# Weight sums in another stage, the residual kept by groups of 768 tokens, and fixed places for the s tiles

## The chip, the cores and the metric

The kernel runs on one core of one Trainium2 chip. The metric is the device time of one execution in microseconds (us); the figure for a kernel is the median of its runs. The core's engines are TensorE (PE in the rows; PEld is its weight load), VectorE (DVE), ScalarE (ACT), GpSimd (POOL) and SyncE (SP), which here issues nearly all transfers, in one order.

## What is computed

Two requests, a prompt of 512 tokens and a sample of 1024, go through the same two layers in fp32: multi-head latent attention, then a chunked gMLP, each with a gate and a residual, and a last norm.

```python
def mla_layer(x, ...):                       # layer 1
    h = rmsnorm(x, g)
    q_lat, kv_lat, k_rope, gate = jnp.split(h @ w_in, [384, 640, 704], axis=-1)
    q  = (rmsnorm(q_lat, q_norm) @ w_q_up)   # 8 heads, 128 + 64
    kv = (rmsnorm(kv_lat, kv_norm) @ w_kv_up)
    ...                                      # rope, softmax over the whole sequence
    return x + (o * jax.nn.silu(gate)) @ w_out

def gmlp_layer(x, ...):                      # layer 2, width 2048
    h = rmsnorm(x, g)
    u, v, gate = jnp.split(h @ w_in, 3, axis=-1)
    u = jax.nn.gelu(u, approximate=False)
    v = layernorm(jax.nn.gelu(v, approximate=False), ln_g, ln_b)
    sv = ...                                 # per group of 256: w_s (128x128) times v, per chunk of 128 tokens
    s = u * sv.reshape(bsz, seq, 2048)
    return x + (s * jax.nn.silu(gate)) @ w_out
```

## The kernel before

Activations lie with channels on the 128 partitions and tokens along the row; a chunk is C = 512 tokens. The sample has the chunks g = 0 and 1, the prompt is g = 2. Every fp32 product is made of three products of a high and a low part: `mm3` multiplies the high weights by the high activations (the first of three lines, L145 in attention, L1232 in the gMLP's output), the high weights by the low activations (the second) and the low weights by the high activations (the third). `split` makes the two parts: ScalarE casts (L150 for activations, L63 for weights) and VectorE subtracts (L151, L64). So before TensorE can use a tile it needs a cast and then a subtract. TensorE turns a matmul of 128x512 around every 0.23 us.

The program is a list of steps; a framework places each instruction in the order of its engine, and from there every engine works in that order.

The stages, with their times in the profile: **a_in_s**, norm and input projection of the sample, 0 to 190 us; attention of the sample to about 575; the prompt's input projection, about 572 to 640; attention of the prompt to 795; **out_s**, the sample's output projection with its residual, to 873; **out_p**, the prompt's, to about 925; then the gMLP. It treats the 1536 tokens as two groups G of 768 (H = 384 is half a group): `b_v` makes v, `b_ug` makes u and the gate and multiplies to s, `b_out` is the output projection, by chunks again: `b_out(0)` from 1302, `b_ug(1)` to 1774, `b_out(1)` and `b_out(2)` from 1774 to 1963.

What the change and the prediction touch:

- **The weight sums.** The gMLP's products are formed by a scheme of seven products of block sums, so sums of blocks of the value weights wv are made once and kept in DRAM (`Sv`). `w_sums(u)` (L810) is one of 16 units: a load of 128x4x256 (`ws<-wv`, L819), four VectorE operations of 128x256 that build on each other (L825), a store (`sv<-ws`, L826). Units 0 to 7 stand in the prompt's input projection, one per step that uses a 'wa' weight; units 8 to 15 in out_s.
- **a_in_s.** `k_step(k, c)` loads a piece x of chunk c, makes its high part on ScalarE (`h_hi`, L287) and its low part on VectorE (`h_lo`, L288), squares it, and adds the squares up on GpSimd (`acc`, L225). TensorE sums the squares over partitions (`ps_st`, L201); VectorE fetches that as `ms` (L203, L163), GpSimd takes the power (`rstd`, L166), and TensorE spreads the result (`ps_bc`, L209), before it goes on.
- **Spread of a norm in the prompt's projection.** `ps_n` (L179, L180) is made from the high and low part (`sh`, `sl`) of a diagonal tile `dg` (L193), which VectorE fills from `rstd`. The rotary part loads a turned copy of the keys there (`rope<-kr`, L343).
- **out_p and the loads of the next group.** `AOut.out` loads a piece of the old residual (`x<-xp`, L746), adds the product to it (L750) and stores the new residual x1 (L751). `b_prep` loads x1 again as `hQ` (L896), in 24 pieces for a group, and spreads the norm as `ps_n` (L916, L917). x1 lies in DRAM as 3 x 8 tiles of 128x512.
- **s and b_out.** `end` (L1132, L1133) stores s to DRAM (`sd<-uo`). `s_load` (L1154) loads a tile of one of the 16 channel blocks d of a chunk into one of five temporary buffers and splits it into `sh`, `sl`. `b_out` runs over the outputs f and the halves u of d: f0u0, f1u0, f2u0, f0u1, and so on, 24 matmuls each. The split tiles live in a rotating pool. For the sample's second chunk three of them, d 0 to 2, are loaded and split within the last unit of `b_ug(1)`, into a pool of their own (`pre`):

```python
        npre = (0, 3)[G]
        b_ug(G, [s_load(G, d, npre) for d in range(npre)])
        step(lambda G=G: open_out(G))
        for d in range(npre, 8):
            step(s_load(G, d, npre))
```

Of the kernel before, what the change touches and what calls it, by code (L numbers as in the profile page):

```python
# [88 lines left out]
def trunk_kernel(tc, A):  # L89
# [293 lines left out]
    def a_in_s():  # L383
        a = AIn("s", 2)

        def begin():
# [346 lines left out]
    class AOut:  # L733
# [9 lines left out]
        def out(self, f, c):  # L743
# [66 lines left out]
    def w_sums(u):  # L810

        vu, kt, hf = u // 8, u // 2 % 4, u % 2
        o = slice(hf * 256, hf * 256 + 256)

        def load():
            t = st["wsum", u] = st["ws"].tile([128, 4, 256], F32, tag="ws", bufs=3 - vu, name="ws")
            nc.sync.dma_start(out=t, in_=A["wv"][vu][:, :, kt, o])  # L819

        def make():
# [325 lines left out]
    def s_load(g, d, pre=0):  # L1147
        def fn():
            x = tmp("s")
            t0 = g * C  # L1150
            while t0 < (g + 1) * C:
                G, o = divmod(t0, 2 * H)
                n = min(2 * H - o, (g + 1) * C - t0)
                nc.sync.dma_start(out=x[:, t0 - g * C:t0 - g * C + n], in_=st["sd", G, d][:, o:o + n])  # L1154
                t0 += n
            hl = [st["pre"].tile([128, C], F32R, name=f"s{e}{d}") if d < pre else
                  st["po"].tile([128, C], F32R, tag="s" + e, bufs=24 if g else 16, name="s" + e)
                  for e in "hl"]
            split(hl[0], hl[1], x)
            st["sf", g, d] = hl  # L1160
# [131 lines left out]

    def open_sums():
        if ("v2d", 0) not in st:
            b_dram()
        st["ws"] = open_pool("ws", side="right")

    def sums_at(n, us):

        if 0 <= n - 2 < len(us):  # L1300
            step(w_sums_of[us[n - 2]][1])
        if 0 <= n < len(us):
            step(w_sums_of[us[n]][0])

    w_sums_of = [w_sums(u) for u in range(16)]
# [22 lines left out]
    def open_out1():  # L1328
# [219 lines left out]
```

## Time and profile before

| | us |
|---|---|
| median of three runs | 1964.0 (1963.76, 1964.0, 1965.2) |
| profiled execution, its own time | 1964.92 |
| its span in the trace | 1963.1 |
| PE busy | 1918.7 (98% of the span) |
| DVE busy | 1294.8 (66%) |
| ACT busy | 889.9 (45%) |
| POOL busy | 140.6 (7%) |
| mean granted clock of TensorE | 0.991 of full |

The profiled execution is 0.9 us above the median of the runs. TensorE is busy for nearly the whole span, so the time is its work plus the few places where it waits, plus the places where its granted clock falls to half: such a stretch shows as 0.50 in the column PEclk of the windows, 1.2 GHz in place of 2.4. A matmul that is busy at half clock counts as busy, so the lost time there is not in the 2% of idle time.

### The profile page before, as it was taken

What the parts mean: (1) busy time and instruction counts of PE and PEld (TensorE: products, weight loads), DVE (VectorE), ACT (ScalarE), POOL (GpSimd) and SP (SyncE); (2) the same over time, 40 slices, a digit from 0 to 9 for tenths busy, and PEclk for the clock granted to TensorE, in tenths of its full rate; (3) what the DMA queues carried; (4) which work ended last, traced back from release to release, by engine and by line L of the source; (5) the groups of instructions that cost most, each with busy time, mean ns of one, the idle gap of its engine ahead of it and who ended that gap; (6) DMA issues with size and microseconds to landing.
All of it is one profiled execution on the core that took longest, in us unless ns stands there. A gap on an engine that the chain in (4) does not pass through costs nothing.

```text
span 1963.1 us, 26564 instructions
## 1 busy us (share of the span) xinstructions
PE 1918.7 (98%) x10226; PEld 1696.1 (86%) x10226; DVE 1294.8 (66%) x1990; ACT 889.9 (45%) x1382; POOL 140.6 (7%) x99
## 2 busy tenths in 40 slices
PE   8999999999998999998999999999999999999998
PEld 6888888888886888886889999988888999998887
DVE  7443777777877787747758777766655665656443
ACT  5322544454543555323544544553444454545321
POOL 5100000000011000122000000001100000000111
PEclk9999999999998999998999999989999999999999
DMA  5211000000126311765557655466575555546443
GB/s 162 86 39 58 27 13 22 17 28 17 38 77 213 107 47 63 235 226 188 183 169 237 199 183 182 157 208 199 160 257 187 190 171 186 165 137 224 167 166 102
DMA packets 127342, 269.42 MB, mean 137 GB/s; under 512 B 12400, under 2 KB 54896, under 8 KB 127216
## 3 DMA queue, kind: packets, MB, share of 16 engines
q1 hardware_dynamic: 127216, 267.73, 42.2%
q8 instruction: 80, 1.31, 0.3%
q14 instruction: 46, 0.38, 0.1%
HBM read 198.74 MB, written 65.01 MB: 134 GB/s over the span
## 4 chain that ended last, share of the span: by engine, by line
PE 85%; DVE 7%; DMA 4%; issue 2%; ACT 1%; POOL 0%; SPq 0%; POOLq 0%; DVEq 0%; ACTq 0%
PE s L595 9%; PE mm L145 7%; PE mm L146 7%; PE mm L147 7%; PE X L984 6%; PE X L985 6%; PE X L986 6%; PE mm L1233 4%; PE mm L1232 4%; PE mm L1234 4%; PE pst L627 3%; PE Z L985 3%; PE Z L984 3%; PE Z L986 3%; PE sv L1118 2%; PE o L146 2%
## 5 line engine op out<-in xcount | busy, mean ns | idle before, releaser
L63 ACT CAST w_hi<-w_raw 128x1024 fp32r<-128x1024 f32 (+3 forms) x267 | 261.0, 978 | 383.2 <-PE mm L146 101.9
L64 DVE TENSOR_TENSOR w_lo<-w_raw,w_hi 128x1024 fp32r<-128x1024 f32 (+3 forms) x267 | 304.5, 1141 | 187.3 <-ACT w_hi L63 186.7
L225 POOL TENSOR_TENSOR acc<-acc,sq 128x512 f32<-128x512 f32 x70 | 115.7, 1654 | 1456.5 <-ACT sq L223 574.8
L1233 PE MATMUL mm<-sl,w_hi 128*128 128x512 f32 (+1 forms) x416 | 157.0, 377 | 2.9 <-DVE sl L151 2.9
L1232 PE MATMUL mm<-sh,w_hi 128*128 128x512 f32 (+1 forms) x416 | 156.3, 376 | 1.9 <-ACT sh L150 1.9
L1234 PE MATMUL mm<-sh,w_lo 128*128 128x512 f32 (+1 forms) x416 | 156.5, 376 | 0.0
L610 ACT ACTIVATE p<-s,sm 128x1024 f32<-128x1024 f32 (+1 forms) x96 | 93.3, 974 | 103.9 <-DVE sm L606 103.8
L150 ACT CAST pth<-pst 128x512 fp32r<-128x512 f32 x160 | 86.5, 591 | 67.2 <-PE pst L627 65.2
L145 PE MATMUL mm<-h_hi,w_hi 128*128 128x512 f32 x288 | 114.8, 399 | 1.0 <-ACT rbc L310 0.9
L147 PE MATMUL mm<-h_hi,w_lo 128*128 128x512 f32 x288 | 113.2, 393 | 0.0
L146 PE MATMUL mm<-h_lo,w_hi 128*128 128x512 f32 x288 | 113.1, 393 | 0.0
L604 DVE TENSOR_REDUCE sm<-s 128x1 f32<-128x1024 f32 (+1 forms) x80 | 97.6, 1220 | 19.5 <-PE s L595 19.4
L151 DVE TENSOR_TENSOR ptl<-pst,pth 128x512 fp32r<-128x512 f32 x160 | 104.7, 683 | 8.4 <-ACT pth L150 8.3
L994 ACT COPY t<-X 128x384 f32<-128x384 f32 (+1 forms) x88 | 44.5, 511 | 126.0 <-PE X L986 125.1
L1233 PEld LDWEIGHTS mm<-sl,w_hi 128*128 128x128 f32 x416 | 79.1, 190 | 18.5 <-DVE sl L151 4.6
L1232 PEld LDWEIGHTS mm<-sh,w_hi 128*128 128x128 f32 x416 | 79.2, 190 | 16.3 <-ACT sh L150 2.2
L1234 PEld LDWEIGHTS mm<-sh,w_lo 128*128 128x128 f32 x416 | 79.2, 190 | 13.9
L146 PE MATMUL o<-ptl,vh 128*128 128x256 f32 x320 | 91.1, 285 | 0.0
L147 PE MATMUL o<-pth,vl 128*128 128x256 f32 x320 | 91.0, 284 | 0.0
L145 PE MATMUL o<-pth,vh 128*128 128x256 f32 x320 | 90.2, 282 | 0.0
L984 PE MATMUL X<-gbh,w_hi 128*128 128x384 f32 x256 | 85.9, 335 | 3.3 <-DVE uo L1083 3.2
L984 PE MATMUL X<-gah,w_hi 128*128 128x384 f32 x256 | 86.9, 339 | 0.0
(292 smaller groups left out, 5112.5 us busy)
## 6 DMA issues: line engine op xcount, KB each, us to landing
w_raw<-wbo SPq DMA_DIRECT2D x50, 512.0 KB, 3.4
w_raw<-wug SPq DMA_DIRECT2D x48, 512.0 KB, 4.4
w_raw<-sv SPq DMA_DIRECT2D x32, 512.0 KB, 3.7
su<-su SPq DMA_DIRECT2D x32, 512.0 KB, 4.1
w_raw<-su SPq DMA_DIRECT2D x32, 512.0 KB, 4.8
w_raw<-wa SPq DMA_DIRECT2D x25, 512.0 KB, 3.6
w_raw<-wv SPq DMA_DIRECT2D x24, 512.0 KB, 3.6
v2d<-c SPq DMA_DIRECT2D x48, 256.0 KB, 2.5
```

The lines of the kernel that those rows point to most:

```text
L63: self.nc.scalar.copy(hi[:, :n], raw[:, :n])
L64: self.nc.vector.tensor_tensor(out=lo[:, :n], in0=raw[:, :n], in1=hi[:, :n].bitcast(F32), op=ALU.subtract)
L145: pe.matmul(out, lh, rh, start=(i == 0), stop=False)
L146: pe.matmul(out, lh, rl, start=False, stop=False)
L147: pe.matmul(out, ll, rh, start=False, stop=(i == n - 1))
L595: pe.matmul(s[:, j2 * C:(j2 + 1) * C], l[:, o], r[:, cc], start=(j == 0), stop=(j == 4))
L984: pe.matmul(ps, lh, rh, start=first, stop=False, skip_group_check=True)
L985: pe.matmul(ps, lh, rl, start=False, stop=False, skip_group_check=True)
L986: pe.matmul(ps, ll, rh, start=False, stop=last, skip_group_check=True)
L1232: pe.matmul(ps, wh[:, ksl(kk)], sh, start=(k == 0), stop=False)
L1233: pe.matmul(ps, wh[:, ksl(kk)], sl, start=False, stop=False)
L1234: pe.matmul(ps, wl[:, ksl(kk)], sh, start=False, stop=(k == 15))
```

## The change

- **Sums.** `w_sums` has 8 units of 128x4x512 in place of 16 of 128x4x256. The first four are moved from the prompt's input projection to a_in_s (`sums_at` after `k_step(k, 1)` from k = 2 on, one at every second step, and on into the steps that follow); the other four stay in out_s, at every third step, with one buffer. The pool `ws` is opened at the start of a_in_s, and the pool of the latents takes its place at (f, c) = (5, 0).
- **Residual.** x1 lies in DRAM as 2 x 8 tiles of 128x768, one for each group G. `by_group` cuts a range of tokens at the group's bound. The stores of the sample's second chunk and the loads of it in `b_out(1)` come in two pieces; the `hQ` loads of a group are 8 of 128x2x384 in place of 24.
- **s tiles.** They get fixed places by tags, allocated in `open_out` in an order that puts d 4 to 12 over memory of h2b, 0 to 3 over `vin` and `sv`, and 13 to 15 over `sv` and `uo`. For g = 2, d 0 to 7 get places of their own, and d 8 to 15 the places 0 to 7. The early load and split of three tiles in the last unit of `b_ug(1)` and their pool are gone; d 0 to 7 are all loaded after `open_out`.

```diff
     def w_sums(u):
-        vu, kt, hf = u // 8, u // 2 % 4, u % 2
-        o = slice(hf * 256, hf * 256 + 256)
+        vu, kt = divmod(u, 4)
         def load():
-            t = st["wsum", u] = st["ws"].tile([128, 4, 256], F32, tag="ws", bufs=3 - vu, name="ws")
-            nc.sync.dma_start(out=t, in_=A["wv"][vu][:, :, kt, o])
+            t = st["wsum", u] = st["ws"].tile([128, 4, C], F32, tag="ws", bufs=2 - vu, name="ws")
+            nc.sync.dma_start(out=t, in_=A["wv"][vu][:, :, kt, :])
...
         for k in range(KD):
             step(k_step(k, 1))
+            sums_at(k - 2, 0, 2)
             if k == 2:
                 step(lambda: a.stats1(0))
...
                 step(lambda f=f, c=c: a.mm(f, c), ("wa", f))
+                sums_at(2 * f + c, 0, 2)
+                if (f, c) == (5, 0):
+                    step(open_lats)
...
+    def sums_at(n, u0, every):
+        u, i = divmod(n, every)
+        if i == 0 and 0 <= u < 4:
+            step(w_sums_of[u0 + u][0])
+        u, i = divmod(n - 2, every)
+        if i == 0 and 0 <= u < 4:
+            step(w_sums_of[u0 + u][1])
...
-    n = 0
-    for s in mm_p[1:2] + mm_p[3:]:
-        step(*s)
-        if len(s) > 1 and s[1][0] == "wa":
-            if n == 0:
-                step(open_sums)
-            sums_at(n, range(8))
-            if n == 9:
-                step(lambda: close_pool("ws"))
-            n += 1
+    steps(mm_p[1:2] + mm_p[3:])
...
-            nc.sync.dma_start(out=st["x1d", g, f], in_=x)
+            for d, o in by_group("x1d", f, g * C, C):
+                nc.sync.dma_start(out=d, in_=x[:, o])
...
-                    t0, t1 = 2 * H * G, 2 * H * (G + 1)
-                    while t0 < t1:
-                        g, o = divmod(t0, C)
-                        h, q = divmod(t0 - 2 * H * G, H)
-                        n = min(C - o, H - q, t1 - t0)
-                        nc.sync.dma_start(out=Q[k][:, j + 2 * h, q:q + n],
-                                          in_=st["x1d", g, k + 4 * j][:, o:o + n])
-                        t0 += n
+                    nc.sync.dma_start(out=Q[k][:, j:j + 3:2, :], in_=st["x1d", G, k + 4 * j].rearrange(
+                        "p (a b) -> p a b", a=2))
...
-            unit(2 * p + 1, AF.Silu, g, early if p == 7 else ((), (), norm_v(p + 1)))
+            unit(2 * p + 1, AF.Silu, g, ((), (), norm_v(p + 1)) if p < 7 else ())
...
+    def s_tiles(g, d):
+        i = d if g < 2 else d + 16 if d < 8 else d - 8
+        st["sf", g, d] = [st["po"].tile([128, C], F32R, tag=f"s{e}{i}", bufs=1, name="s" + e) for e in "hl"]
...
+        for d in (*range(4, 13), *range(4), *range(13, 16)):
+            s_tiles(G, d)
...
-        npre = (0, 3)[G]
-        b_ug(G, [s_load(G, d, npre) for d in range(npre)])
+        b_ug(G)
         step(lambda G=G: open_out(G))
-        for d in range(npre, 8):
-            step(s_load(G, d, npre))
+        for d in range(8):
+            step(s_load(G, d))
```

How the orders of two engines change at three places. First, VectorE in a_in_s while the last pieces of the second chunk are split (`h_lo`) and the norm's sum is fetched (`ms`). Before:

```order
L151 TENSOR_TENSOR w0lo<-w0raw,w0hi 128x128 x3
L288 SCALAR_TENSOR_TENSOR h_lo_1_342<-x,vec,h_hi_1_341 128x512
L288 SCALAR_TENSOR_TENSOR h_lo_1_360<-x,vec,h_hi_1_359 128x512
L288 SCALAR_TENSOR_TENSOR h_lo_1_378<-x,vec,h_hi_1_377 128x512
L288 SCALAR_TENSOR_TENSOR h_lo_1_406<-x,vec,h_hi_1_405 128x512
L288 SCALAR_TENSOR_TENSOR h_lo_1_424<-x,vec,h_hi_1_423 128x512
L288 SCALAR_TENSOR_TENSOR h_lo_1_454<-x,vec,h_hi_1_453 128x512
L288 SCALAR_TENSOR_TENSOR h_lo_1_463<-x,vec,h_hi_1_462 128x512
L288 SCALAR_TENSOR_TENSOR h_lo_1_472<-x,vec,h_hi_1_471 128x512
L203 COPY ms<-ps_st 128x4
```

After, the end of the same piece:

```order
L299 SCALAR_TENSOR_TENSOR h_lo_1_412<-x,vec,h_hi_1_411 128x512
L844 TENSOR_TENSOR ws<-ws 128x512
L299 SCALAR_TENSOR_TENSOR h_lo_1_430<-x,vec,h_hi_1_429 128x512
L844 TENSOR_TENSOR ws<-ws 128x512
L299 SCALAR_TENSOR_TENSOR h_lo_1_460<-x,vec,h_hi_1_459 128x512
L299 SCALAR_TENSOR_TENSOR h_lo_1_478<-x,vec,h_hi_1_477 128x512
L844 TENSOR_TENSOR ws<-ws 128x512 x4
L299 SCALAR_TENSOR_TENSOR h_lo_1_515<-x,vec,h_hi_1_514 128x512
L299 SCALAR_TENSOR_TENSOR h_lo_1_524<-x,vec,h_hi_1_523 128x512
L844 TENSOR_TENSOR ws<-ws 128x512
L299 SCALAR_TENSOR_TENSOR h_lo_1_540<-x,vec,h_hi_1_539 128x512
L203 COPY ms<-ps_st 128x4
```

Seven operations of the sums stand in this piece between the `h_lo` and ahead of `ms`, and an eighth just ahead of the piece.

Second, VectorE in the prompt's input projection, from the key's scaling (`kr`) to the diagonal tile `dg` that the spread of the norm needs. Before:

```order
L336 TENSOR_TENSOR kr<-mm,rbc_5589 128x512
L64 TENSOR_TENSOR w_lo<-w_raw,w_hi 128x1024
L825 TENSOR_TENSOR ws<-ws 128x256 x4
L64 TENSOR_TENSOR w_lo<-w_raw,w_hi 128x1024
L186 TENSOR_TENSOR dg<-ps_n,ident 128x512
L825 TENSOR_TENSOR ws<-ws 128x256
L188 TENSOR_REDUCE ms<-dg 128x4
L163 TENSOR_SCALAR ms<-ms 128x4
L193 TENSOR_TENSOR dg<-ident,rstd 128x512
```

After:

```order
L347 TENSOR_TENSOR kr<-mm,rbc_5608 128x512
L64 TENSOR_TENSOR w_lo<-w_raw,w_hi 128x1024
L186 TENSOR_TENSOR dg<-ps_n,ident 128x512
L64 TENSOR_TENSOR w_lo<-w_raw,w_hi 128x1024
L188 TENSOR_REDUCE ms<-dg 128x4
L163 TENSOR_SCALAR ms<-ms 128x4
L193 TENSOR_TENSOR dg<-ident,rstd 128x512
```

The five operations of the sums are gone from between, and `dg` stands ahead of the second weight split.

Third, TensorE where `b_ug(1)` ends and `b_out(1)` begins. Before (a number behind a name tells buffers apart, and `sh0`, `sh1`, `sh2` are d 0 to 2):

```order
L986 MATMUL X_15820<-gbh_12782,w_lo_15866 128x384
L1232 MATMUL mm_16010<-sh0_15838,w_hi_15907 128x512 [waits PE_49]
L1233 MATMUL mm_16010<-sl0_15839,w_hi_15907 128x512
L1234 MATMUL mm_16010<-sh0_15838,w_lo_15908 128x512
L1232 MATMUL mm_16010<-sh1_15859,w_hi_15907 128x512
L1233 MATMUL mm_16010<-sl1_15860,w_hi_15907 128x512
L1234 MATMUL mm_16010<-sh1_15859,w_lo_15908 128x512
L1232 MATMUL mm_16010<-sh2_15886,w_hi_15907 128x512
L1233 MATMUL mm_16010<-sl2_15887,w_hi_15907 128x512
L1234 MATMUL mm_16010<-sh2_15886,w_lo_15908 128x512
L1232 MATMUL mm_16069<-sh0_15838,w_hi_15941 128x512 [waits Activation_49]
```

After:

```order
L999 MATMUL X_15729<-gbh_12691,w_lo_15761 128x384
L1244 MATMUL mm_15935<-sh_15875,w_hi_15795 128x512 [waits PE_49,Activation_49]
L1245 MATMUL mm_15935<-sl_15876,w_hi_15795 128x512 [waits DVE_49]
L1246 MATMUL mm_15935<-sh_15875,w_lo_15796 128x512
L1244 MATMUL mm_15935<-sh_15877,w_hi_15795 128x512 [waits Activation_49]
L1245 MATMUL mm_15935<-sl_15878,w_hi_15795 128x512 [waits DVE_49]
L1246 MATMUL mm_15935<-sh_15877,w_lo_15796 128x512
L1244 MATMUL mm_15935<-sh_15879,w_hi_15795 128x512 [waits Activation_49]
L1245 MATMUL mm_15935<-sl_15880,w_hi_15795 128x512 [waits DVE_49]
```

Before, TensorE goes through the three tiles for f0, f1 and f2 in turn without a wait for a split; after, it takes all eight tiles of f0 first, and each waits for its cast and its subtract.

## Rows read from the trace of the kernel before

**Rows 1.** The page's first part, busy time, share of the span and count of each engine, and the first line of the chain of work that ended last, its share by engine.

```profile
PE 1918.7 (98%) x10226; PEld 1696.1 (86%) x10226; DVE 1294.8 (66%) x1990; ACT 889.9 (45%) x1382; POOL 140.6 (7%) x99
...
PE 85%; DVE 7%; DMA 4%; issue 2%; ACT 1%; POOL 0%; SPq 0%; POOLq 0%; DVEq 0%; ACTq 0%
```

**Rows 2.** The waits of TensorE over the whole span: engine, what waited and its line, what it waited for, us in total, times, longest us.

```profile
PE ps_n L916 <- ACT sh L150: 7.1, 2, 6.7
...
PE ps_n L179 <- ACT sh L150: 3.8, 2, 2.6
...
PE mm L1233 <- DVE sl L151: 2.9, 3, 1.3
PE ps_n L180 <- DVE sl L151: 2.4, 3, 1.6
PE mm L1232 <- ACT sh L150: 1.9, 1, 1.9
```

**Rows 3.** Windows: from:to, length, then busy time and count of PE, PEld, DVE, ACT and POOL, granted clock, DMA share, GB/s.

```profile
50.00:190.00 140.00, 140.00 (x680) 118.05 (x679) 55.61 (x84) 38.51 (x56) 11.25 (x9) 1.00 0.20 64
...
626.87:637.10 10.23, 8.02 (x17) 5.12 (x18) 10.23 (x16) 6.18 (x9) 0.00 (x0) 0.50 0.18 54
893.11:903.34 10.23, 5.80 (x13) 4.20 (x14) 5.96 (x8) 2.87 (x6) 1.27 (x1) 0.50 0.57 203
1306.12:1316.35 10.23, 8.24 (x18) 5.55 (x19) 5.99 (x10) 3.11 (x6) 0.00 (x0) 0.50 0.91 288
```

**Rows 4.** Timeline of a_in_s, 24 to 44 us: start, duration (of a run of several: from its first start to its last end), engine, line, operation, count, and in brackets the idle time of the engine before it and what ended that.

```profile
24.11 0.74 DVE L288 SCALAR_TENSOR_TENSOR h_lo<-x,vec,h_hi 128x512 fp32r<-128x512 f32 x1
...
25.59 7.81 POOL L225 TENSOR_TENSOR acc<-acc,sq 128x512 f32<-128x512 f32 x5 [1.56 <-DVE sq L221]
...
27.07 9.53 DVE L288 SCALAR_TENSOR_TENSOR h_lo<-x,vec,h_hi 128x512 fp32r<-128x512 f32 x8
...
36.52 0.15 DVE L203 COPY ms<-ps_st 128x4 f32<-128x4 f32 x1
...
36.95 1.02 POOL L166 TENSOR_TENSOR rstd<-ms,mhalf 128x4 f32<-128x4 f32 x1 [3.55 <-DVE ms L163]
...
38.03 1.16 PE L209 MATMUL ps_bc<-ident,rstd 128*128 128x128 f32 x8
```

**Rows 5.** Timeline of the prompt's input projection, 612 to 632 us, with the same columns.

```profile
612.68 1.22 DVE L64 TENSOR_TENSOR w_lo<-w_raw,w_hi 128x1024 fp32r<-128x1024 f32 x1
...
615.90 4.12 SPq L343 DMA_DIRECT2D rope<-kr  x4
...
618.51 1.06 ACT L63 CAST w_hi<-w_raw 128x1024 fp32r<-128x1024 f32 x1 [4.82 <-PE mm L146]
...
619.40 1.35 DVE L825 TENSOR_TENSOR ws<-ws 128x256 f32<-128x256 f32 x3 [5.18 <-DMA ws<-wv]
...
624.75 0.69 DVE L193 TENSOR_TENSOR dg<-ident,rstd 128x512 f32<-128x512 f32 x1 [1.13 <-POOL rstd L166]
...
626.75 0.71 PE L179 MATMUL ps_n<-sh,onesr 128*128 128x512 f32 x1 [2.61 <-ACT sh L150]
...
629.04 0.80 PE L180 MATMUL ps_n<-sl,onesr 128*128 128x512 f32 x1 [1.58 <-DVE sl L151]
...
631.78 0.80 PE L145 MATMUL mm<-h_hi,w_hi 128*128 128x512 f32 x1
```

**Rows 6.** Timeline of out_p, 881 to 897 us, with the same columns.

```profile
881.28 8.53 SPq L896 DMA_DIRECT2D hQ<-x  x18
...
889.85 0.43 SPq L746 DMA_DIRECT2D x<-xp  x1
...
890.71 1.23 DVE L64 TENSOR_TENSOR w_lo<-w_raw,w_hi 128x1024 fp32r<-128x1024 f32 x1 [4.25 <-ACT w_hi L63]
...
894.61 0.69 DVE L750 TENSOR_TENSOR x<-mm,x 128x512 f32<-128x512 f32 x1 [2.67 <-DMA x<-xp]
...
896.48 0.69 PE L916 MATMUL ps_n<-sh,onesr 128*128 128x384 f32 x1 [6.70 <-ACT sh L150]
```

**Rows 7.** Timeline of the start of `b_out(0)`, 1304 to 1318 us, with the same columns.

```profile
1304.72 0.50 PE L1232 MATMUL mm<-sh,w_hi 128*128 128x512 f32 x1 [1.90 <-ACT sh L150]
...
1306.55 0.80 PE L1233 MATMUL mm<-sl,w_hi 128*128 128x512 f32 x1 [1.33 <-DVE sl L151]
...
1312.68 0.80 PE L1233 MATMUL mm<-sl,w_hi 128*128 128x512 f32 x1 [1.14 <-DVE sl L151]
...
1313.60 3.41 ACT L150 CAST sh<-s 128x512 fp32r<-128x512 f32 x5 [6.86 <-DMA s<-sd]
```

**Rows 8.** Timeline of the start of `b_out(1)`, 1774 to 1788 us, with the same columns.

```profile
1774.35 0.39 PE L1232 MATMUL mm<-sh,w_hi 128*128 128x512 f32 x1
...
1775.76 2.69 ACT L150 CAST sh<-s 128x512 fp32r<-128x512 f32 x5
...
1777.52 3.10 DVE L151 TENSOR_TENSOR sl<-s,sh 128x512 fp32r<-128x512 f32 x5
...
1778.24 8.31 SPq L1154 DMA_DIRECT2D s<-sd  x12
...
1784.12 0.62 ACT L150 CAST sh<-s 128x512 fp32r<-128x512 f32 x1 [5.67 <-DMA s<-sd]
...
1785.96 2.06 ACT L150 CAST sh<-s 128x512 fp32r<-128x512 f32 x3 [0.27 <-DMA s<-sd]
```

More of the change, by code (lines that the diff above doesn't have):

```diff
@@ L231, in new_acc, with by_group @@
         return st["ap"].tile([128, C], F32, tag="acc", bufs=st["acc_n"], name="acc")
+    def by_group(name, f, t0, n):
+        out, a = [], t0
+        while a < t0 + n:
+            G, o = divmod(a, 2 * H)
+            m = min(2 * H - o, t0 + n - a)
+            out.append((st[name, G, f][:, o:o + m], slice(a - t0, a - t0 + m)))
+            a += m
+        return out
     def setup():
@@ L254, in setup @@
         act.copy(st["mhalf"], st["mhalf"])
-        for g in range(3):
+        for G in range(2):
             for k in range(KD):
-                st["x1d", g, k] = st["dram"].tile([128, C], F32, name=f"x1_{g}_{k}")
+                st["x1d", G, k] = st["dram"].tile([128, 2 * H], F32, name=f"x1_{G}_{k}")
     step(setup)
@@ L387, in begin @@
             st["gp", "s"] = open_pool("gates", side="right")
-            st["lp", "s"] = open_pool("lats", side="right")
+            st["ws"] = open_pool("ws", side="right")
+            b_dram()
             st["krp", "s"] = open_pool("krs")
@@ L395, in begin, with open_lats @@
                 st["aps", "s", f, 0] = mm_tile()
+        def open_lats():
+            close_pool("ws")
+            st["lp", "s"] = open_pool("lats", side="right")
         step(begin)
@@ L825, in make @@
                 dve.tensor_tensor(out=t[:, r, :], in0=t[:, a, :], in1=t[:, b, :], op=op)
-            nc.sync.dma_start(out=st["Sv", vu][:, :, kt, o], in_=t)
+            nc.sync.dma_start(out=st["Sv", vu][:, :, kt, :], in_=t)
         return load, make
@@ L1058, in b_v, with b_ug @@
         return out
-    def b_ug(G, early):
+    def b_ug(G):
         def load_v(p):
@@ L1143, in b_ug, with s_load @@
                 step(mix(p, u, e))
-            unit(2 * p + 1, AF.Silu, g, early if p == 7 else ((), (), norm_v(p + 1)))
+            unit(2 * p + 1, AF.Silu, g, ((), (), norm_v(p + 1)) if p < 7 else ())
             step(end(p, u, g))
-    def s_load(g, d, pre=0):
+    def s_tiles(g, d):
+        i = d if g < 2 else d + 16 if d < 8 else d - 8
+        st["sf", g, d] = [st["po"].tile([128, C], F32R, tag=f"s{e}{i}", bufs=1, name="s" + e) for e in "hl"]
+    def s_load(g, d):
         def fn():
             x = tmp("s")
[L1150 to L1160, printed above, removed]
+            for s, o in by_group("sd", d, g * C, C):
+                nc.sync.dma_start(out=x[:, o], in_=s)
+            if g == 2:
+                s_tiles(g, d)
+            split(*st["sf", g, d], x)
         return fn
@@ L1226, in out @@
                 st["xr", f] = tmp("xr")
-                nc.sync.dma_start(out=st["xr", f][:, :n], in_=st["x1d", g, f][:, o])
+                for d, q in by_group("x1d", f, g * C + o.start, n):
+                    nc.sync.dma_start(out=st["xr", f][:, q], in_=d)
             ps = st["ops", f][:, :n]
@@ L1276, in b_out @@
         return [fin0, fin1, fin2], [[lambda f=f, fn=fn: fn(f) for f in range(KD)] for fn in (fin3, fin4)]
+    w_sums_of = [w_sums(u) for u in range(8)]
+    def sums_at(n, u0, every):
[5 more added lines that the diff above has]
+            step(w_sums_of[u0 + u][1])
     def steps(lst):
@@ L1290, in trunk_kernel @@
     main_s(weave, [mm_p[0], mm_p[2]])
[L1293 to L1305, printed above, removed]
-    n = 0
-    for s in mm_p[1:2] + mm_p[3:]:
-        step(*s)
-        if len(s) > 1 and s[1][0] == "wa":
-            if n == 0:
-                step(open_sums)
-            sums_at(n, range(8))
-            if n == 9:
-                step(lambda: close_pool("ws"))
-            n += 1
+    steps(mm_p[1:2] + mm_p[3:])
     out_s, out_p = AOut("s", 2, 0), AOut("p", 1, 2)
@@ L1331, in open_out1 @@
         st["go_pool"] = open_pool("outs1")
-        open_sums()
+        st["ws"] = open_pool("ws", side="right")
     step(open_out1)
@@ L1340, in trunk_kernel @@
                 step(lambda f=f, c=c: out_s.out(f, c), ("wao", f))
-                sums_at(2 * f + c - 3, range(8, 16))
-                if 2 * f + c == 13:
+                sums_at(2 * f + c - 3, 4, 3)
+                if 2 * f + c == 14:
                     step(lambda: close_pool("ws"))
@@ L1413, in trunk_kernel @@
     for G in range(2):
-        step(open_in)
+        step(lambda G=G: open_in(G))
         for i, s in enumerate(b_v(G)):
```

5 lines of the change are left out of this document (3 added, 2 removed).

## The prediction

> **What bounds the kernel now.** I read the page's busy times and its chain first: TensorE is busy 98% of the span, and the chain lies on it for 85% [rows 1]. So an edit on another engine is worth only what it changes of TensorE's waits and of its clock. The list of TensorE's waits gives where these are [rows 2], and the windows give the clock: after some of the waits a stretch of 10.23 us runs at 0.50, which is 1.2 GHz [rows 3]. In each of the three, TensorE had waited in the few microseconds before. The change touches three of these places (the prompt's projection at 627 us, out_p at 893, the start of `b_out(0)` at 1306), and two where TensorE now waits hardly at all (a_in_s around 38 us, the start of `b_out(1)` at 1774). I go through the five in order of time. In a stage where TensorE never idles, as from 50 to 190 us (140.00 of 140 us busy [rows 3]), time lost ahead of it is not won back.
>
> **a_in_s: the sums that arrive, +5.4 us.** After the change, eight VectorE operations of 128x512 stand among the `h_lo` and ahead of `ms`. VectorE has no room there: its eight `h_lo` fill 27.07 to 36.60, and `ms` starts at 36.52 [rows 4]. From `ms` a chain runs without slack to TensorE: `rstd` on GpSimd ends at 37.97, `ps_bc` on TensorE starts at 38.03 [rows 4]. A single 128x512 of VectorE takes about 0.69 us, and independent ones follow each other by 0.60 (five in 3.10 [rows 8]). The sums build on each other, and the old ones show no overlap (three in 1.35 where one takes 0.42 [rows 5]), so I take 0.68: 8 x 0.68 = 5.4 us, and `ps_bc` at 43.4 instead of 38.03. Bounds: nothing, if VectorE still finishes before TensorE asks; +10, since `h_lo` takes 0.74 alone and up to 1.7 while GpSimd's five adds run from 25.59 to 33.40 [rows 4], and a sum there would do the same. I take no extra for that, since the five adds are five in either case and each holds up whichever VectorE operation stands beside it. The loads and stores of two units go through SP's queue ahead of x pieces and weights; the weights are needed only some 8 us after `ps_bc`, so I cost that at nothing, and at some 2 us if the cover is gone.
>
> The Trainium skill (page "SBUF — State Buffer", section "SBUF: two separate sides") speaks of this pair: VectorE and GpSimd share a port pair, taken as an exclusive lock for a whole instruction while the other blocks. The slow `h_lo` agree with that. By it the five adds are paid for once, and the term stays; if every sum were as slow as the `h_lo` beside GpSimd, the term would be 8 x 1.7 = 13.6 us and the total about 1977.
>
> **The prompt's projection: the sums that leave, -8.7 us.** TensorE waits for `sh` and `sl` of `ps_n` there (3.8 and 2.4 us, [rows 2]): at 626.75, 629.04 and once more before 631.78 [rows 5]. Then it runs at half clock until 637.10 [rows 3]. The loss against a stage without waits is 4.8 us of waits plus about 4.6 of half clock (the rest of the 10.23 us at half speed), 9.5 in all. The chain behind it is VectorE's: it sat 5.18 us for the load of a sum unit (`ws`, 619.40), with the weight split, `dg` and `ms` queued behind, so that the later `dg` came at 624.75 [rows 5]. Without sums, `dg`, a weight split (1.22) and `ms` follow the weight split of 612.68 [rows 5] at once and are done by about 616.3, and with `rstd` the later `dg` is by about 618.3. Then `sh` waits on ScalarE only for the cast that TensorE releases at 618.51 and that ends at 619.57 [rows 5], so `sh` is there at about 620.2. Next late is `sl`: ahead of it stand the rotary steps, which need the `rope` loads. Their 4.12 us of issues began at 615.90 behind the unit's load and store [rows 5]; without these they begin about 1.5 us earlier, land by about 620.5, and `sl` is done at about 624.1. TensorE asks for it at about 624.2. The second pair is ready at about 625, a wait of 0.8. So 9.5 - 0.8 = 8.7 gained, if 0.8 us of idle leaves the clock alone. Bounds: -9.5 (no wait at all), and -5 (the waits go but the clock still falls).
>
> **out_p: fewer `hQ` issues, -1.4 us.** The load `x<-xp` stands behind 18 `hQ` issues of 8.53 us (881.28 to 889.81) and TensorE waits 6.70 us for what follows from it at 896.48 [rows 6]. With 8 larger issues, three before the store and five after, `x<-xp` goes out about 5 us earlier and lands at about 889. But the next thing on VectorE is a weight split from 890.71 to 891.94 [rows 6], so the add starts at about 891.9 in place of 894.61: 2.7 us less wait, 4.0 left. The clock fell at 893.11, 3.3 us after TensorE had run dry, so 4.0 still reaches it. The stretch of 10.23 us is the same, and what TensorE starts earlier in it runs at half speed: half of 2.7 is 1.4. Bounds: 0, and -6.1 if the clock stays up (the 2.7, and half of the 6.86 us from 896.48 to the end of the stretch).
>
> **Start of `b_out(0)`: about 0.** Fixed places take a wait for a store away from VectorE, but TensorE's waits there, 1.90, 1.33 and 1.14 [rows 7], hang on the casts and the subtracts after the last unit, and on the sixth tile's load, whose cast started at 1313.60 after 6.86 us of idle [rows 7]. That load now stands behind two `hQ` transfers of 393 KB, 786 KB against 384 before, on the same queue. Bounds: -3 (the wait for the store was the last) and +2 (the larger transfers are).
>
> **Start of `b_out(1)`: the early splits go, +9.1 us.** Before, 27 matmuls of f0, f1, f2 on the tiles d 0 to 2 bridge 1774.35 to 1780.5 while d 3 to 7 are cast from 1775.76 and subtracted from 1777.52 to 1780.62 [rows 8]; TensorE doesn't wait. After, f0 starts with d 0, whose cast and subtract come no sooner than those of d 3 did: first matmul at about 1776.4, second at about 1778.2, the pattern of 1.90 and 1.33 of `b_out(0)` [rows 7]. The five temporary buffers hold d 0 to 4, so d 5 takes the place in the queue that d 8 has now, issued at 1778.24, cast at 1784.12 [rows 8]. Its subtract ends at about 1785.5, those of d 6 and 7 follow as the three casts from 1785.96 do, and f0 ends at about 1788.7. Before, 24 matmuls at 0.227 us from 1774.35 end at 1779.8. That is 8.9 lost. The same step of `b_out(0)` has this course already: there f0 goes from 1302.8 to 1317.7 [rows 7], 14.9 us in place of 5.45, or 9.4. I take the middle, +9.1. Half clock mostly falls into the waits, as it does there. Bounds: +4 (only the first waits, 1.90 + 1.33 + 1.14 [rows 7], and d 5 earlier), and +12 (3 us of half clock behind f0). Nothing hides it, since `b_out(1)` and `b_out(2)` are TensorE's to the end.
>
> **The rest, 0 to +3.** The sums in out_s, the eight added stores, the split loads of `xr` and the wait of the last eight tiles of g = 2 for their places stand beside TensorE's work with some 20 us to spare; I take 0.
>
> **Sum.** 5.4 - 8.7 - 1.4 + 0 + 9.1 + 0 = +4.4. The durations are from an execution of 1964.92 (span 1963.1), which becomes 1969.3; against the median of 1964.0 it is **1968.4**.
>
> **Rivals.**
> - **Half clock in a_in_s too (1972.5, slower).** The wait before `ps_bc` comes in pieces of 0.7 to 2.9 us. If they set off a stretch at 0.50 as in the three windows [rows 3], of its 10.23 us some 2 fall into the waits, and half of the other 8.2 is 4.1: 1968.4 + 4.1. For it speaks that the loss of 5.4 is more than the 3.3 after which the clock fell in out_p; against it that TensorE works between the pieces. [...]
> - **The wait in the projection stays (1977.1, slower).** The sums were then not its cause, and another step ends last (the `rope` loads or the weight cast). Against it: 5.18 us of VectorE idle with `ws` named [rows 5].
> - **The sums in a_in_s are hidden (1963.0, same).** For it: the casts in that stage wait for x at times; against: `ms` stood right behind the last `h_lo` [rows 4].
> - **The loss at `b_out(1)` doesn't come (1959.3, faster).** If fixed places let the loads of d 0 to 2 and their splits slip ahead of the last unit's, the change doesn't do what it says there. Against it: the order puts the casts behind the unit.
> - **The clock stays full in out_p (1963.7, same).**
>
> **How the numbers follow.** A measurement of this kernel can tell about 0.2%, or 3.9 us: faster is below 1960.1, slower above 1967.9. Chances: the forecast (1965.5 to 1971.5) 0.50, of which a bit under half lies within 0.2%; half clock in a_in_s 0.17; the wait stays 0.05; sums hidden 0.10; no loss at `b_out(1)` 0.10; full clock in out_p 0.05; others, faster, 0.03. Faster is 0.10 + 0.03 = 0.13; same is 0.10 + 0.05 + 0.24 = 0.39; slower is 0.26 + 0.17 + 0.05 = 0.48. The range goes from 1960.5 to 1975: it leaves out the loss that doesn't come, the wait that stays and the others, 0.18 together.
>
> **What the profile after would show.** `ps_bc` at about 43.4; no wait over 1 us for `ps_n` near 625 and a clock of 1.00 there; the wait for `ps_n` in out_p at about 4 us, followed by 0.50; the first matmul of `b_out(1)` waiting about 1.9 us, and f0 ending about 14 us after it is due to start. The prediction is wrong if `ps_bc` moves by less than 2 us, if the clock still falls at 627, or if `b_out(1)` starts without a wait.

## The result, and the profile after

| | before | after |
|---|---|---|
| median, us | 1964.26 (four runs, 1963.76 to 1965.2) | 1983.49 (1980.59 to 1986.33, four runs) |
| profiled execution, own time | 1964.92 | 1985.3 |
| its span | 1963.1 | 1983.5 |
| mean granted clock | 0.991 | 0.987 |

The ratio is 1.0097 (95% interval 1.008 to 1.0115): the change makes the kernel 19 us slower, where 4.4 were forecast. The forecast time of 1968.4 and its range up to 1975 both lie below every run.

The page of the kernel after, busy times and the first line of the chain (the answer to [rows 1]):

```profile
PE 1928.0 (97%) x10226; PEld 1704.6 (86%) x10226; DVE 1287.7 (65%) x1958; ACT 890.3 (45%) x1382; POOL 141.9 (7%) x99
...
PE 86%; DVE 6%; DMA 4%; issue 1%; ACT 1%; SPq 0%; POOL 0%; DVEq 0%; POOLq 0%; ACTq 0%
```

TensorE has the same 10226 matmuls and is busy 9.3 us longer (half clock counts as busy); the other 11 us of the 20.4 in the span are waits. The waits of TensorE after the change (the answer to [rows 2]; engine, what waited, for what: us in total, times, longest):

```profile
PE mm L1244 <- ACT sh L150: 7.7, 4, 2.5
PE ps_n L179 <- ACT sh L150: 7.2, 2, 6.1
...
PE ps_n L929 <- ACT sh L150: 4.2, 2, 3.9
PE X L997 <- DVE uo L1096: 3.8, 2, 3.2
PE X L997 <- DVE x L770: 3.1, 1, 3.1
...
PE ps_bc L209 <- POOL rstd L166: 2.6, 1, 2.6
PE mm L1245 <- DVE sl L151: 2.8, 3, 1.3
```

The 6.1 of `ps_n` L179 is a new one: it begins at 868.75, at the end of out_s, and not in the prompt's projection, where it stood before. The 3.1 for `x` L770 is new as well. The windows show where the clock fell (columns as in [rows 3]):

```profile
29.05:32.46 3.41, 3.41 (x8) 2.66 (x9) 3.41 (x4) 1.60 (x3) 3.25 (x3) 0.50 0.84 285
623.00:635.00 12.00, 11.91 (x53) 9.51 (x52) 10.77 (x18) 8.07 (x11) 0.00 (x0) 1.00 0.16 54
872.14:878.97 6.83, 4.15 (x9) 3.03 (x10) 3.84 (x6) 2.83 (x4) 1.79 (x2) 0.50 0.37 112
899.45:906.28 6.83, 6.23 (x15) 4.75 (x16) 4.76 (x7) 2.83 (x5) 1.11 (x1) 0.50 0.41 146
933.58:940.41 6.83, 6.16 (x15) 4.85 (x16) 6.83 (x8) 3.85 (x6) 2.92 (x2) 0.50 0.35 120
1312.46:1319.29 6.83, 5.56 (x13) 4.13 (x13) 3.90 (x7) 1.74 (x4) 0.00 (x0) 0.50 0.97 315
1541.16:1547.98 6.82, 6.02 (x22) 6.02 (x23) 4.21 (x9) 3.64 (x5) 0.00 (x0) 0.50 0.34 115
1790.33:1793.74 3.41, 3.07 (x7) 2.48 (x8) 2.69 (x5) 0.53 (x2) 0.00 (x0) 0.50 1.01 293
```

The projection (623 to 635) now runs without a wait at 1.00. Five stretches are new: in a_in_s (29.05), at the end of out_s (872.14), at the start of `b_v(0)` (933.58), at the start of `b_ug(1)` (1541.16) and at the start of `b_out(1)` (1790.33).

Since TensorE has the same count of matmuls in every kernel here, a stage can be cut at the starts of the same two of them. Here "A" is the change alone in the profile above, and the other columns are the runs told of below (us longer than before's profile in that stage; stages that differ by under 1 in all columns are left out):

| stage (time before) | length before | A | sums_only | resid_only | tiles_only | bank_fix | old_out_s | sums_late | best |
|---|---|---|---|---|---|---|---|---|---|
| a_in_s, to 55 us | 55.41 | +5.42 | +7.12 | +0.75 | +0.29 | +7.02 | +5.77 | +1.13 | +0.27 |
| prompt's projection, 612 to 657 | 45.44 | -9.15 | -9.15 | +0.47 | -1.20 | -9.16 | -9.16 | -9.15 | -9.16 |
| end of out_s, 860 to 885 | 25.44 | +8.41 | +7.35 | 0.00 | +1.95 | +10.00 | 0.00 | +7.97 | 0.00 |
| out_p, 885 to 916 | 30.89 | -2.32 | -1.29 | -1.56 | -0.37 | -3.43 | -0.95 | -2.35 | -2.14 |
| start of `b_v(0)`, 916 to 948 | 31.76 | +6.24 | +3.70 | 0.00 | 0.00 | 0.00 | +6.20 | 0.00 | 0.00 |
| start of `b_ug(0)`, 14 us long | 13.82 | -0.50 | -0.65 | -0.23 | +0.37 | +2.34 | -0.85 | +0.81 | +2.44 |
| the rest of `b_ug(0)` | 228.85 | -0.01 | -0.01 | +2.01 | +0.91 | -0.01 | +0.51 | +0.44 | +1.04 |
| start of `b_out(0)`, 33 us long | 33.15 | +1.13 | +0.10 | +1.00 | -1.41 | +1.15 | +1.31 | +0.88 | +1.13 |
| `b_v(1)` | 86.85 | +0.28 | +0.35 | +0.02 | +1.15 | +0.63 | +0.57 | +0.60 | +0.73 |
| start of `b_ug(1)`, 20 us long | 19.95 | +3.90 | +0.04 | +1.41 | +0.74 | +2.12 | +0.48 | +1.81 | +1.00 |
| start of `b_out(1)`, 33 us long | 32.76 | +7.39 | 0.00 | 0.00 | +7.19 | +7.49 | +8.07 | +8.31 | 0.00 |
| span | 1963.1 | 1983.5 | 1970.3 | 1967.2 | 1972.1 | 1981.5 | 1973.9 | 1973.5 | 1959.1 |

The experiments ran in five sessions, in which the medians of the kernel before were 1964.3, 1967.4, 1969.9, 1968.8 and 1967.3 us. So a time is compared with before in its own session, and the stages tell more than the total: those that hang on a transfer's landing, or on whether half clock follows a wait, vary by 1 to 3 us, the others repeat within 0.1.

### The profile page after: what moved, and what is told of

Its sections match the earlier page's. It is cut to its first block, busy times and chain, and to the rows that moved or that the text cites. A ratio compares the mean times of both kernels' runs of the same rounds, so it can differ in the third digit from the quotient of the medians.

```text
span 1983.5 us, 26483 instructions
## 1 busy us (share of the span) xinstructions
PE 1928.0 (97%) x10226; PEld 1704.6 (86%) x10226; DVE 1287.7 (65%) x1958; ACT 890.3 (45%) x1382; POOL 141.9 (7%) x99
## 3 DMA queue, kind: packets, MB, share of 16 engines
q8 instruction: 80, 1.31, 0.3%
## 4 chain that ended last, share of the span: by engine, by line
PE 86%; DVE 6%; DMA 4%; issue 1%; ACT 1%; SPq 0%; POOL 0%; DVEq 0%; POOLq 0%; ACTq 0%
PE s L615 9%; PE X L997 6%; PE X L998 6%; PE X L999 6%; PE mm L145 6%; PE mm L146 6%; PE mm L147 6%; PE mm L1244 4%; PE mm L1245 4%; PE mm L1246 4%; PE pst L647 3%; PE Z L997 3%; PE Z L998 3%; PE Z L999 3%; PE sv L1131 2%; PE o L146 2%
```

## The experiments

**The parts alone.** Three kernels, each the one before with one of the three parts of the diff.

> The kernel before with the weight sums' part of the change alone. Theory 1 (the sums carry most of the loss, at places that have nothing to do with the residual): a_in_s +5.5, the prompt's projection -9.3, the end of out_s +8 (TensorE waits some 6 us for the norm of the sample there, then half clock), the first matmul of b_v(0) waits 3 us for VectorE and drops to half clock, +6: 1964.3 + 10.2 = about 1974.5, with no wait at the start of b_out(1). Rival (the losses at out_s and b_v(0) come from the stores in two pieces and the larger hQ loads): 1964.3 + 5.5 - 9.3 = 1960.5.

> The kernel before with the residual in groups of 768 tokens alone. Theory 1: the wait in out_p falls from 6.70 to about 4 us, -2.8; the start of b_out(0) costs about 1 more; 1962 to 1963. Rival (the pieces and the larger loads are what delays out_s and b_v(0)): +8 to +14 at these two, 1970 or more.

> The kernel before with the s tiles in fixed places and without the early splits alone. Theory 1: +7.4 at the start of b_out(1), nothing elsewhere: about 1971.7. Rival (fixed places take other waits away, at b_out(0) and for g = 2, and pay for it): 1964 to 1967. If the wait at the start of b_ug(1) grows past 3 us here and its clock falls, 4 more: then that loss hangs on the memory places of this part and not on chance.

Measured: sums_only 1976.0 (ratio 1.0043, interval 1.0028 to 1.0058), resid_only 1970.21 (1.0009, 0.9994 to 1.0023), tiles_only 1976.68 (1.0053, 1.0036 to 1.0069). By the stages theory 1 holds for the place of each part: the sums carry a_in_s, the projection, the end of out_s and `b_v(0)`; the tiles carry `b_out(1)`; the residual's 1.56 in out_p is eaten by others. Not all sizes came as expected: `b_v(0)` lost 3.70 in sums_only and not 6, since the wait of 3.42 us was not followed by half clock there, and the wait in out_p was 5.41 in resid_only and not about 4. The spans of the three are 7.2, 4.1 and 9.0 us above before's, 20.3 together beside 20.4 for the whole change, though the single stages do not add up so closely. At the end of out_s and in `b_v(0)` resid_only loses nothing, so the stores in pieces are not the cause there.

**The bank of the first X.** In the order of TensorE the first matmul of `b_v(0)` waits for VectorE only after the change. Its result X is the first tile of a new PSUM pool and lies in bank 0. The last product of out_p lay in bank 1 before and lies in bank 0 after. The four banks of the old pool are handed out as they come free, and from the first `ps_bc` of a_in_s on, banks 0 and 1 are swapped.

```diff
         st["ps"], st["mm"] = open_pool("psumb", space=bass.MemoryType.PSUM), "y"
+        bank("Y")
```

> The changed kernel, with one line more: an unused tile of the other kind is taken first in the gMLP's PSUM pool, so that the X tiles lie in banks 4 to 7. In the built program the first X tile of b_v(0) lay in bank 0 with the last product of out_p, where before that product was in bank 1. Theory 1: the wait of 3.07 us of the first X matmul for VectorE's add goes, and the half clock after it: 1983.5 - 6.2 = about 1977. Rival (another step, the cast or subtract of the input, ends just as late, and the bank is not what it waits for): 1982 to 1984.

Of the kernel after, TensorE's row at the wait; then of bank_fix the rows of the same place, timelines of TensorE:

```profile
934.25 0.77 PE L997 MATMUL X<-w_hi,gah 128*128 128x512 f32 x1 [3.07 <-DVE x L770]
```

```profile
932.86 0.39 PE L147 MATMUL mm<-goh,w_lo 128*128 128x512 f32 x1
933.09 0.39 PE L997 MATMUL X<-w_hi,gah 128*128 128x512 f32 x1
```

The wait is gone, X follows 0.23 us behind the last product, and the stage is back at 31.76 us exactly, 6.24 less. The total was 1983.5 all the same (ratio 1.0084 beside 1.0097): in that profile a_in_s and the end of out_s took 3.2 us more, and the start of `b_ug(0)` 2.8. The last is a wait of 1.89 us for the first v tile and 3.41 us of half clock behind it; that wait was 0.63 in the kernel after, 1.14 in before and 1.69 when the kernel after was run once more, so whether the 2.8 belongs to the bank is not shown. The price of the bank is shown by its stage, not by the total.

**out_s as before.** The four units of 1 MB go back to eight of 512 KB with two buffers, one per step.

```diff
...
-                sums_at(2 * f + c - 3, 4, 3)
-                if 2 * f + c == 14:
+                sums_at(2 * f + c - 3, 4, 1, 8)
+                if 2 * f + c == 13:
```

> The changed kernel with the four units of out_s as before (eight of 128x4x256, two buffers, one per step). Theory 1 (the 1 MB unit with a single buffer arrives late, VectorE stands waiting for it, and the adds of the residual queue behind): the stage from the middle of out_s to the start of out_p falls from 33.9 to about 26 us, and the kernel by 8, to about 1975 beside a changed kernel of 1983.5. Rival (the stores in two pieces delay the chain of x loads and stores): it stays above 31.

1979.13 in a session where before took 1969.87 (1.0046, 1.0031 to 1.0062); the stage is 25.44, as before, and the wait for `ps_n` L179 is gone. It is out_s's units. Theory 1 had VectorE's wait for the last unit as the reason, which the next run tried.

```diff
-            for r, a, b, op in ((3, 2, 3, ALU.add), (2, 0, 2, ALU.subtract),
...
+            for r, a, b, op in () if u == 7 else (
+                    (3, 2, 3, ALU.add), (2, 0, 2, ALU.subtract),
...
```

> The changed kernel without the four VectorE sums of the last unit of out_s; its load and its store are kept, so a quarter of the second sum matrix is not summed. Theory 1 (VectorE's wait for this one unit is the loss): the stage at the end of out_s at 25.5 to 27 us, no wait over 2 us of ps_n there. Rival (the transfers of 1 MB on the queue ahead of the x loads are the loss): 31 or more, as with the sums.

1990.61 (one run): the stage takes 34.03 without those sums, so theory 1 falls. VectorE's adds of the residual, timeline of no_last_sums:

```profile
849.09 0.69 DVE L770 TENSOR_TENSOR x<-mm,x 128x512 f32<-128x512 f32 x1 [4.06 <-DMA x<-xs]
857.79 0.69 DVE L770 TENSOR_TENSOR x<-mm,x 128x512 f32<-128x512 f32 x1 [4.83 <-DMA x<-xs]
863.61 0.69 DVE L770 TENSOR_TENSOR x<-mm,x 128x512 f32<-128x512 f32 x1 [5.12 <-DMA x<-xs]
868.71 0.69 DVE L770 TENSOR_TENSOR x<-mm,x 128x512 f32<-128x512 f32 x1 [4.41 <-DMA x<-xs]
```

Each add waits for the piece `x<-xs` of the old residual, and each piece is issued only behind the store of the piece before. That is a chain of load, add, store and load, with little to spare against the 24 matmuls (5.45 us) of a step. Where the 1 MB load is in flight, 8.7 us pass from add to add, and 9.2 in the kernel after (847.50 to 856.66), against 3.8 to 5.2 in before (849.38, 854.57, 859.05, 863.59, 867.42). So a theory 2: the late 1 MB loads slow the pieces. With one buffer a unit's load can't go before the store of the unit before has landed (the stores land at 829.56 and 845.16, the loads go at 829.62 and 845.22), which puts two loads into the last 45 us before the wait's end.

```diff
-            nc.sync.dma_start(out=t, in_=A["wv"][vu][:, :, kt, :])
+            q = nc.sync if vu == 0 else nc.gpsimd
+            q.dma_start(out=t, in_=A["wv"][vu][:, :, kt, :])
```

> The changed kernel with the loads of out_s's four sum units issued from GpSimd's queue instead of SyncE's; the same bytes and the same work on VectorE. Theory 2 (the pieces x<-xs of the residual are a chain of load, add, store, load, and a piece that is issued behind a 1 MB unit on the one queue lands after it, 7 to 8 us in place of 4): the pieces land in 3 to 5 us and the stage at the end of out_s falls from 33.9 to 26 to 28. Rival (all queues share the transfer engines, so the megabyte costs the same from any queue): 32 to 34. Theory 1 (VectorE's wait for the last unit) was refuted by the run without those sums.

1992.68 (one run), the stage 39.05. The transfers of other_queue that start from 820 to 872 us (operation, count, KB each, median us to landing):

```profile
x<-xs SPq DMA_DIRECT2D x8, 256.0 KB, 4.4
...
ws<-wv POOLq DMA_DIRECT2D x2, 1024.0 KB, 7.0
```

The loads took 7.0 us from GpSimd's queue, and the two pieces beside them landed 6.5 and 5.3 us after their issue, so the place in one queue is not what delays them: in that the rival holds, though the stage is 5 us longer than it had. Why it is worse than the changed kernel was not tried apart; GpSimd's adds of squares that follow the two loads waited for their squares and not for the loads.

In half_loads, units 5 and 7 are neither loaded nor summed, and units 4 and 6 are stored twice.

> The changed kernel with only the first and the third unit of out_s loaded and summed; each is stored twice, so the second and fourth quarter of that sum matrix hold copies of others. Theory 2: of the two residual pieces that land 4 us late in the changed kernel the one behind the fourth unit's load is on time again, and the stage falls by about half of the loss, to 28 to 30. Rival (the 1 MB stores, which stay, are what delays the pieces): 33 to 34.

1978.43 (one run); the stage takes 27.05, only 1.6 above before and less than the 28 to 30 expected. The last load is now issued at 818.75 and has landed at 827.38, while the kernel after issues its last two at 829.62 and 845.22. The transfers that start from 820 to 872 us, in before, after and half_loads (operation, count, KB each, median us to landing):

```profile
x<-xs SPq DMA_DIRECT2D x10, 256.0 KB, 3.9
ws<-wv SPq DMA_DIRECT2D x4, 512.0 KB, 4.6
```

```profile
x<-xs SPq DMA_DIRECT2D x8, 256.0 KB, 3.8
ws<-wv SPq DMA_DIRECT2D x2, 1024.0 KB, 8.5
```

```profile
x<-xs SPq DMA_DIRECT2D x9, 256.0 KB, 3.6
```

The median of the pieces hides it: in the kernel after two of the eight took 8.03 and 6.79 us (issued at 832.68 and 848.59, 3 us behind the two loads), where none of the ten in before took over 4.81. The 1 MB stores were kept in half_loads, and the last unit's sums alone changed nothing in no_last_sums, so it is the late loads. They bring no more bytes than before: the rows show four loads of 512 KB there and two of 1 MB after. What differs is the size of each, and that one buffer lets the last one go only at 845.22; old_out_s takes both back, and they were not tried apart.

**The sums later in a_in_s.** Two units are loaded only after the first norm is spread (a copy of one column on ScalarE into the tile holds the load back), and the other two go to the first four steps of the projection.

```diff
+            if u < 2:
+                act.copy(t[:, 0, 0:1], st["rbc", "s", 0][:, 0:1])
+            nc.sync.dma_start(out=t, in_=A["wv"][vu][:, :, kt, o])
...
```

> The changed kernel with two of the four early units in a_in_s, their loads held back until the norm of the first chunk is spread (one small copy on ScalarE more for each), and the other two as four units of 128x4x256 in the first steps of the prompt's projection. Theory 1 (the loss in a_in_s is that the sums stand ahead of ms): a_in_s within 1 us of before (55.4 to its 200th matmul), the projection still about 36.3 in place of 45.4, and the last product of out_p is in bank 1 again in the built program, so that the first X matmul doesn't wait: 1983.5 - 5.4 - 6.2 = about 1972. Rival (the sums cost what they cost wherever they stand in a_in_s): a_in_s at 60 or more. Rival 2 (any unit in the projection brings its wait back): 45.

1975.0 in a session with before at 1969.87 (1.0029, 1.0018 to 1.0041). a_in_s is at +1.13, the projection keeps its -9.15, and in `b_v(0)` nothing is lost: with VectorE's old order ahead of `ms` the banks fall as before. Both rivals fall.

**What is left, put together.** The residual's part, the sums as in sums_late, out_s's units and the early splits as before.

> The kernel before with the residual in groups of 768 tokens and the sums as in the run with two late units, but with out_s's units as before and the s tiles with their early splits as before. Theory 1 (four separate losses, each of which is taken away here): projection -9, out_p -2 to -3, the start of b_out(0) +1, the rest as before: about 10 us below the kernel before on the same chip, 1954 to 1958. Rival (TensorE's next wait takes the place of each): within 4 us of before.

> As the best run, but with the residual as before, in pieces of 512 tokens. Open: whether the residual's part is worth its place. By the stages of the part runs it gains 1.5 to 2.3 us in out_p and loses 1 at the start of b_out(0): then this run stands within 2 us above the best one, relative to before a ratio of 0.995 to 0.997. Rival (the larger hQ transfers slow other loads of the gMLP, where the part run with the residual alone showed +2): this one is faster, 0.993 or less.

best: 1960.26 beside 1969.87 (0.995, 0.9932 to 0.9969), the 10 us expected and faster than both kernels. The gain in the projection stays whole, and 2.14 in out_p. Little of the 2.14 is wait: TensorE still waits 6.01 us there, beside 6.70 in before, and the stretch of half clock is 6.83 us long in place of 10.23. The start of `b_ug(0)` gives 2.4 back and `b_out(0)` 1.1. best_no_resid: 1961.85 beside 1967.28 (0.9964, 0.9953 to 0.9975). The intervals overlap, so whether the residual's part is worth anything stays open.

**The change once more.**

> The changed kernel again, unaltered. Open: whether the 3.9 us at the start of b_ug(1), which none of the part runs showed beyond 2, belongs to the kernel. If it hangs on when the first v tile lands, it varies from run to run between 0 and 4 here; if it belongs to the combination of the parts, it stands at 3.9 again. The other stages should repeat: a_in_s +5 to +7, projection -9.15, end of out_s +8.4, b_v(0) +6.2, b_out(1) +7.4.

1985.59 beside 1968.81 (1.0081, 1.0061 to 1.0101). The stages repeat within 1.5 us, and the start of `b_ug(1)` stands at +3.50.

## Why the prediction was wrong

**The projection was right.** Forecast -8.7, measured -9.15 in every run with the sums moved, and 0.50 is gone from there. The 0.8 us of wait that the forecast left there did not come. Of the 3.8 us that it reads from [rows 2] for `ps_n` L179, 1.19 stand at 1415.41 and not in the projection, but the 4.8 it reckons with are right.

**a_in_s was right in size.** Eight sums ahead of `ms` put `ps_bc` at 43.4 by the forecast. The timeline after:

```profile
29.03 1.76 DVE L844 TENSOR_TENSOR ws<-ws 128x512 f32<-128x512 f32 x1
...
30.72 1.76 DVE L299 SCALAR_TENSOR_TENSOR h_lo<-x,vec,h_hi 128x512 fp32r<-128x512 f32 x1
...
36.70 2.73 DVE L844 TENSOR_TENSOR ws<-ws 128x512 f32<-128x512 f32 x4
...
41.93 0.15 DVE L203 COPY ms<-ps_st 128x4 f32<-128x4 f32 x1
...
43.44 1.16 PE L209 MATMUL ps_bc<-ident,rstd 128*128 128x128 f32 x8 [2.57 <-POOL rstd L166]
```

A sum beside GpSimd's add takes 1.76 like an `h_lo`, four without it 2.73, or 0.68 each. The five adds slow five operations, whichever they are (here two `w0lo`, two sums and an `h_lo`; in before a `w0lo` and four `h_lo`), so the term of 5.4 held. It measured 5.42 to 5.77 in four of the eight profiles with the sums there, and 6.85 to 7.12 in the four where a stretch of half clock lies at `ps_bc` as well (from 43.54 us in sums_only): the rival's mechanism, at 1.5 us and not 4.1. The stretch at 29.05, after a wait of 2.03 for `w0lo`, stands ahead of VectorE's chain, which set the end. That sums_late loses only 1.1 shows the cause.

**out_p was right in the wait, off in the clock.** Forecast 4.0 us of wait, measured 3.88; but the clock fell 5.0 us after TensorE had run dry (894.45 to 899.45) and not 3.3, and the stretch of 0.50 was 6.83 us long and not 10.23, so -2.3 and not -1.4. The wait hangs on an order of VectorE that the forecast took from the rows of before: weight split, add, `dg`. The kernel after keeps it, and the split hides that the piece landed 1.0 us after TensorE had run dry, not 0.8 ahead of it. In resid_only the add comes first, then the split, then `dg`, and the wait is 5.41. VectorE, first in the kernel after, then in resid_only:

```profile
895.38 1.23 DVE L64 TENSOR_TENSOR w_lo<-w_raw,w_hi 128x1024 fp32r<-128x1024 f32 x1 [4.25 <-ACT w_hi L63]
896.52 0.68 DVE L770 TENSOR_TENSOR x<-mm,x 128x512 f32<-128x512 f32 x1
897.12 0.55 DVE L917 TENSOR_TENSOR dg<-ident,r 128x384 f32<-128x384 f32 x1
```

```profile
892.41 0.69 DVE L761 TENSOR_TENSOR x<-mm,x 128x512 f32<-128x512 f32 x1 [4.77 <-DMA x<-xp]
893.02 1.22 DVE L64 TENSOR_TENSOR w_lo<-w_raw,w_hi 128x1024 fp32r<-128x1024 f32 x1
894.15 1.62 DVE L910 TENSOR_TENSOR dg<-ident,r 128x384 f32<-128x384 f32 x1
```

old_out_s and best have the second order as well, with waits of 6.10 and 6.01. So there is luck in the 4.0: the residual's part brings the piece forward in all of them, and the order on VectorE decides what TensorE gets of it.

**`b_out(1)` was right, somewhat too dear.** Forecast +9.1, measured +7.39. The rows after:

```profile
1788.84 0.50 PE L1244 MATMUL mm<-sh,w_hi 128*128 128x512 f32 x1 [1.90 <-ACT sh L150]
...
1790.67 0.80 PE L1245 MATMUL mm<-sl,w_hi 128*128 128x512 f32 x1 [1.34 <-DVE sl L151]
...
1796.24 2.04 ACT L150 CAST sh<-s 128x512 fp32r<-128x512 f32 x3 [5.38 <-DMA s<-sd]
...
1796.91 0.50 PE L1244 MATMUL mm<-sh,w_hi 128*128 128x512 f32 x1 [1.33 <-ACT sh L150]
```

The first waits are the 1.90 and 1.33 of [rows 7], as forecast; d 5 to 7 came in one run of casts, and the half clock was short, so f0 ended 12.7 us after it was due to start and not 14. tiles_only and best show that the third part of the change is all of it; the fixed places went with the early splits in both, and that it is the splits rests on these rows and the order of TensorE. `b_out(0)` lost 1.1 where 0 was forecast, within its bounds.

**The step that failed is "the rest, 0 to +3".** It said that the sums in out_s "stand beside TensorE's work with some 20 us to spare". I had read the stage's busy times and not its chain: the pieces of the residual follow each other with hardly any slack, and a load of 1 MB in their way costs it. That is +8.41, of which 6.07 are wait. The wait of `X` for the bank (+6.24, of which 3.07 are wait) was in no term and no rival. It stood in the order of TensorE after the change, as one more semaphore at the first `X`, and I had not compared the waits there, since no line of the diff touches that place. Third, the start of `b_ug(1)`: +3.90. TensorE waits 3.20 us there for the first v tile (2.06 before), which lands 1.1 us later, and 6.83 us of half clock follow, where none did before. VectorE's wait for that tile, before and after:

```profile
1528.22 2.03 DVE L1069 TENSOR_SCALAR vin<-vin,mv 128x256 f32<-128x256 f32 x6 [5.45 <-DMA vin<-v2d]
```

```profile
1538.27 2.03 DVE L1082 TENSOR_SCALAR vin<-vin,mv 128x256 f32<-128x256 f32 x6 [6.59 <-DMA vin<-v2d]
```

The three make 18.55 of the 20.4 us between the two spans. The terms that were named come to 2.5 (5.42 - 9.15 - 2.32 + 1.13 + 7.39), against 4.4 forecast.

**What stays open.** Why the first v tile lands later, whether that comes from the change at all, and why half clock follows some waits and not others. From issue to landing that tile took 7.1 to 9.0 us in the fourteen profiles, 7.3 in before and 8.4 and 7.9 in the two of the change. All parts together showed 3.5 and 3.9, no part alone more than 1.4, and the kernels with most of the parts 0.5 to 3.4. Bytes and order on the queue are the same as before there; where the tiles lie in DRAM was not tried. Why other_queue is worse than the changed kernel is open too.

## What to carry to other kernels

A stage with busy engines and idle time on each can still have no slack: follow the chain of its loads, adds and stores, and ask what a larger transfer beside it does to each link. When work is moved between stages, compare the waits in the two built programs along the whole of the bound engine, since a pool's buffers can be handed out in another order far from the edit. And a step that is fed early only to bridge a stage's start (three tiles here) is worth what the start would cost without it, 7 us here for 12 KB per partition.

## What the runs showed of the hardware

- A load of 1 MB took 8.5 us, and 256 KB beside it 6.8 to 8.0 in place of 2.5 to 4.8 in before, from the same queue; issued from another queue, the megabyte took 7.0 and the pieces 5.3 and 6.5. The Trainium skill (page "DMA: Bandwidth & Descriptors", section "Queues, rings and completion order") says that each transfer engine takes turns between the queues that have work for it, packet by packet; the run agrees in that a second queue doesn't take the load out of the way.
- Stretches at 0.50 were 3.41, 6.83 and 10.23 us long. The length of the wait ahead did not tell whether one follows: `X` of `b_v(0)` waited 3.07 us in the kernel after, with 6.83 us at half clock behind it, and 3.42 in sums_only and half_loads, with full clock; at the start of `b_ug(1)` 1.91 us in resid_only were followed by 3.41 us at half clock, and 3.06 in best by full clock.
